# One transformer layer on one core: another scratch place for a norm's squares, late modulation sums made and read in the middle of a product, and block 0's output sums on VectorE

## The chip, the cores and the metric

The kernel runs on one core of a Trainium2 chip. A core has five engines that run side by side, each through its own list of instructions in order: TensorE (PE in the profile, with PEld for the loading of its weights), VectorE (DVE), ScalarE (ACT), GpSimd (POOL) and SyncE (SP), which here only issues transfers (DMA). An instruction waits until the semaphores that it names have been reached, and everything behind it on its engine waits too. Matmuls write their results into PSUM, a small memory of banks; a bank holds 128 x 512 numbers of 32 bits. All else lies in SBUF, in 128 partitions.

The metric is the time of one execution on the device in microseconds (us).

## The reference

The reference is an encoder trunk with one layer: 2048 tokens of 1024 numbers, a mixer and a feed-forward network (FFN), each between two RMS norms, with shift, scale and gate computed from a vector c. With one layer the mixer is stick-breaking attention with 16 heads of 64.

```python
def stick_breaking_mixer(h, w_qkv, w_o):
    qkv = (h @ w_qkv).reshape(b, s, 3, N_HEADS, HEAD_DIM)
    q, k, v = qkv[:, :, 0], qkv[:, :, 1], qkv[:, :, 2]
    for q0 in range(0, s, SB_BLOCK):
        ...
        z = jnp.einsum('bthd,bshd->bhts', q[:, q0:end], k[:, :end]).astype(jnp.float32) * scale
        ...
        sp = jnp.where(mask, jax.nn.softplus(z), 0.0)
        rest = lax.cumsum(sp, axis=3, reverse=True)
        log_a = jnp.where(mask, z - rest, -jnp.inf)
        a = jnp.exp(log_a).astype(v.dtype)
        outs.append(jnp.einsum('bhts,bshd->bthd', a, v[:, :end]))
    o = jnp.concatenate(outs, axis=1).reshape(b, s, D_MODEL)
    return o @ w_o
...
    mod_all = jnp.einsum('bd,lde->lbe', jax.nn.silu(c), ada_w) + ada_b[:, None]
        sh_m, sc_m, gt_m, sh_f, sc_f, gt_f = jnp.split(mod_all[i][:, None, :], 6, axis=-1)
        h = modulate(rms_norm(x, norm_g[i, 0]), sh_m, sc_m)
        y = stick_breaking_mixer(h, sb_w_qkv[r], sb_w_o[r])
        x = x + gt_m * rms_norm(y, norm_g[i, 1])
        h = modulate(rms_norm(x, norm_g[i, 2]), sh_f, sc_f)
        y = swiglu_ffn(h, ffn_w_in[i], ffn_w_out[i])
        x = x + gt_f * rms_norm(y, norm_g[i, 3])
```

The modulation vector has six segments of 1024, numbered 0 to 5: shift, scale and gate of the mixer, then of the FFN. Segments 0 and 1 are needed at the very start, 2 (the mixer's gate) only after the attention, 3 and 4 before the FFN, and 5 at the end.

## The kernel before

Every product of float32 numbers is made of three matmuls: each operand is split into a high and a low part, and high·high, high·low and low·high are summed in one bank (`mm3`, L192 to L194). The tokens are taken in 4 blocks of 512, the heads in 8 pairs p. Names carry these numbers: `pj5_3_0` is the product of pair 5, block 3, kind 0 (0 queries, 1 keys, 2 values), `xT2_0` belongs to block 2.

The order of the work on PE, ACT, DVE and POOL is the order in which the program is written, with generators that are stepped in turn. SP's order of transfers is chosen by a scheduler. The stages by time are: loads, the modulation's first segments and the first products (to about 60 us); projections and attention, interleaved (to about 1390); the output projection (to about 1530); the FFN (to the end).

*The first norm.* The tokens of a block are loaded in four tiles x (`x_load`, L319). ACT squares each tile (`x_square`, L183) and sums the squares along the way; only the sums are used, the squares themselves go to a scratch place (`junk`). DVE then scales the tiles (L340), PE transposes them (xT, L366) and ACT writes the modulated result (hf, L387) from the bank that the transposes filled. Blocks 1 and 3 square in place. Block 2 writes its squares to four tiles xj of the tag "wraw", of which there are two places; the keys and queries of an early pair (kn, qn) have stood in the same places, from which they are stored to memory (k_park L502, q_park L516).

*The attention.* A slot of the loop makes one row of scores: z (L588), its exponentials on ACT (L605, L607), a cumulative sum along the row on DVE (the scans w, L617 and L622), a difference on POOL (a, L629) with carries c (L628), a transpose on PE (t, L639), the split into high and low parts aT (L649 on ACT, L655 on DVE), and the product with the values (o, L667). Between these, PE makes the projections pj of a later block: a product has 8 slices k, three matmuls each, and its result is split by ACT and DVE (kn and qn, L490 and L491) or transposed (vT L530, vt L536, v L540 and L541). One pool of three banks, tag "acc", holds the products pj, the sums o, the transposes vt and the sums ap of the next paragraph; t has two banks, z three.

*Late modulation.* `late_modulation` is a generator that loads the weights of a segment in chunks (aw, L225, into "wraw" places), multiplies and adds them on DVE into aacc, waits `settle` steps, and sums aacc over the partitions by matmuls with a tile of ones into a bank ap. For a gate (segments 2 and 5) it loads rows of constants (gr), adds ap and multiplies on DVE (L296, L297), and stores the row; else it adds to columns (shift L249 or scale). In the attention it runs from slot 120 on, every second slot, for segments 2, 3 and 4; for segment 5 it runs in the FFN, with its tiles in "aT" places.

*Output sums.* The result of the attention is written to memory in two parts (high and low sums). `lead_in` does block 0's share of the output projection's preparation while the attention still runs: each of 8 tiles is loaded (`o_load`, op), its parts are added (`o_add`, of, L1082), and the sum is split (`o_prep`, ohl, L1089 on ACT and L1090 on DVE). It takes tiles 0 to 5 at about 1262 to 1302 us, and tiles 6 and 7 at about 1331 to 1338.

Of the kernel before, what the change touches and what calls it, by code (L numbers as in the profile page):

```python
# [9 lines left out]
F32 = mybir.dt.float32  # L10
F32R = mybir.dt.float32r
AF = mybir.ActivationFunctionType
ALU = mybir.AluOpType
# [107 lines left out]
def hybrid_trunk_kernel(  # L121
# [136 lines left out]

    def late_modulation(segs, tag, n, ahead, waits, pool, ptag, acc_tag="tmp", rows_tag="wraw", settle=3, pace=1):

# [9 lines left out]
        for at, (seg, half, k0) in enumerate(chunks):  # L270
# [13 lines left out]
            if k0 + n < KC:  # L284
                continue
            for _ in range(settle):
                yield
            ps = pool.tile([P, BT], F32, name=f"ap{seg}_{half}", tag=ptag)
            if seg in (2, 5):
                g = seg // 3  # L290
                rows = att.tile([P, 2, BT], F32, name=f"gr{g}_{half}", tag=rows_tag, bufs=BUFS[rows_tag])
                nc.sync.dma_start(rows, gate_consts[g : g + 1, half].to_broadcast((P, 2, BT)))
                nc.tensor.matmul(ps, ones, acc, start=True, stop=True)
                for _ in range(3):
                    yield
                nc.vector.tensor_tensor(rows[:, 0], ps, rows[:, 0], op=ALU.add)  # L296
                nc.vector.tensor_tensor(rows[:, 0], rows[:, 0], rows[:, 1], op=ALU.mult)  # L297
                nc.sync.dma_start(gate_rows[g, :, half * BT : (half + 1) * BT], rows[:, 0])
            else:
                ada_cols([acc], ps, half)  # L300
                yield
                sl = slice(4 * half, 4 * half + 4)
# [25 lines left out]
    def x_square(b, i):  # L328
        junk = x_tiles[b, i]
        if b == 0:  # L330
            junk = x_norm[b, i] = att.tile([P, D], F32, name=f"xn{b}_{i}", tag="kt", bufs=BUFS["kt"])
        elif b == 2:
            junk = att.tile([P, D], F32, name=f"xj{b}_{i}", tag="wraw", bufs=BUFS["wraw"])
        x_rstd[b, i] = rms_scale(att, x_tiles[b, i], f"n0_{b}_{i}", junk=junk)
# [115 lines left out]
    def project(at):  # L450
# [10 lines left out]
        def product(t):  # L461
# [7 lines left out]
            for k in range(KC):  # L469
# [11 lines left out]
                if ahead and k == 6:  # L481
                    split_weights(p + 1, t)
                mm3(acc, (w[0][:, k], w[1][:, k]), (h[k][:, 0], h[k][:, 1]), k == 0, k == KC - 1)
                yield
            return acc
# [465 lines left out]
    products(1, 7)  # L951
    late = late_modulation((2, 3, 4), "wraw", 2, 0, 3, accps, "acc")

# [124 lines left out]
    def o_add(b, k):  # L1078
        parts = o_parts.pop((b, k))
        o = att.tile([P, BT], F32, name=f"of{b}_{k}", tag="tmp", bufs=BUFS["tmp"])  # L1080
        eng = nc.vector if b else nc.gpsimd
        eng.tensor_tensor(o, parts[:, 0], parts[:, 1], op=ALU.add)  # L1082
        o_sum[b, k] = o
# [697 lines left out]
```

## Time and profile before

| | |
|---|---|
| median of 3 runs | 2841.5 us (2839.93, 2841.5, 2845.77) |
| the profiled execution | 2840.45 us |
| its span, first to last instruction | 2838.2 us |
| PE busy | 2798.2 us (99%) |
| DVE busy | 2022.4 us (71%) |
| ACT busy | 1630.7 us (57%) |
| POOL busy | 1282.5 us (45%) |
| mean granted clock of PE | 0.998 |

A row of the timeline gives start, length, engine, line, operation, output and inputs (buffer numbers left out), and the number of instructions that were put together. A bracket at its end gives how long the engine stood idle before it, and what ended the wait. A row of the windows gives a stretch of time, its length, the busy time (and instructions) of PE, PEld, DVE, ACT and POOL, then PE's granted clock, the share of DMA engines at work, and GB/s. A row of grouped instructions gives the shortest, median and longest duration in ns. Busy times count overlapping instructions once.

### The profile page before, as it was taken

What the parts mean: (1) busy time and instruction counts of PE and PEld (TensorE: products, weight loads), DVE (VectorE), ACT (ScalarE), POOL (GpSimd) and SP (SyncE); (2) the same over time, 40 slices, a digit from 0 to 9 for tenths busy, and PEclk for the clock granted to TensorE, in tenths of its full rate; (3) what the DMA queues carried; (4) which work ended last, traced back from release to release, by engine and by line L of the source; (5) the groups of instructions that cost most, each with busy time, mean ns of one, the idle gap of its engine ahead of it and who ended that gap; (6) DMA issues with size and microseconds to landing.
All of it is one profiled execution on the core that took longest, in us unless ns stands there. A gap on an engine that the chain in (4) does not pass through costs nothing.

```text
span 2838.2 us, 41766 instructions
## 1 busy us (share of the span) xinstructions
PE 2798.2 (99%) x13821; PEld 2331.5 (82%) x13821; DVE 2022.4 (71%) x2833; ACT 1630.7 (57%) x3271; POOL 1282.5 (45%) x2032
## 2 busy tenths in 40 slices
PE   9899999999999999999999999999999999999998
PEld 7688888888888888887888888888888888888887
DVE  7788888888888888888866766655775665123376
ACT  5787777787787877877645533333433333322243
POOL 1575666676576655657411222221222222544454
PEclk9999999999999999999999999999999999999999
DMA  9774556656665635546288644334453334545575
GB/s 378 275 226 164 186 163 220 212 179 226 193 210 187 214 115 178 196 134 231 85 304 308 207 138 152 123 94 160 137 178 108 112 108 164 192 140 155 180 226 187
DMA packets 239785, 521.03 MB, mean 184 GB/s; under 512 B 22481, under 2 KB 108497, under 8 KB 222674
## 3 DMA queue, kind: packets, MB, share of 16 engines
q1 hardware_dynamic: 239570, 518.38, 56.2%
q8 instruction: 109, 1.79, 0.3%
q14 instruction: 106, 0.87, 0.1%
HBM read 351.04 MB, written 118.49 MB: 165 GB/s over the span
## 4 chain that ended last, share of the span: by engine, by line
PE 88%; DVE 4%; issue 2%; DMA 2%; ACT 2%; POOL 1%; SPq 0%; DVEq 0%; POOLq 0%; ACTq 0%
PE s L192 9%; PE s L193 9%; PE s L194 9%; PE z L588 8%; PE o L667 8%; PE t L639 8%; PE pj L192 5%; PE pj L194 5%; PE pj L193 5%; PE o L194 5%; PE o L193 5%; PE o L192 5%; PE y L194 2%; PE y L192 2%; PE y L193 2%
## 5 line engine op out<-in xcount | busy, mean ns | idle before, releaser
L629 POOL TENSOR_TENSOR a<-a,w 128x512 f32<-128x512 f32 (+3 forms) x640 | 622.1, 972 | 218.9 <-DVE w L622 128.6
L622 DVE TENSOR_TENSOR_SCAN w<-z,c,begin 128x512 f32<-128x512 f32 x384 | 489.2, 1278 | 83.7 <-ACT z L607 62.0
L192 PE MATMUL s<-r,l 128*128 128x512 f32 x1232 | 481.4, 391 | 1.5 <-ACT p L1456 0.9
L194 PE MATMUL s<-r,l 128*128 128x512 f32 x1232 | 479.6, 389 | 0.0
L193 PE MATMUL s<-r,l 128*128 128x512 f32 x1232 | 479.4, 389 | 0.0
L605 ACT ACTIVATE a<-z 128x512 f32<-128x512 f32 (+3 forms) x640 | 347.1, 542 | 170.0 <-PE z L588 137.3
L667 PE MATMUL o<-aT,v 128*128 128x512 f32 (+3 forms) x1280 | 385.3, 382 | 0.1
L655 DVE TENSOR_TENSOR aT<-t,aT 128x512 fp32r<-128x512 f32 (+3 forms) x640 | 358.4, 593 | 24.3 <-ACT aT L649 23.7
L588 PE MATMUL z<-kt,qt 128*128 128x512 f32 (+3 forms) x1280 | 363.6, 365 | 0.0
L649 ACT CAST aT<-t 128x512 fp32r<-128x512 f32 (+3 forms) x640 | 313.9, 533 | 73.6 <-PE t L639 63.5
L607 ACT ACTIVATE z<-z 128x512 f32<-128x512 f32 (+3 forms) x640 | 344.8, 539 | 0.0
L1520 POOL TENSOR_TENSOR one<-p,p 128x512 f32<-128x512 f32 x44 | 70.6, 1606 | 574.5 <-issue 321.8
L192 PE MATMUL pj<-ht,w 128*128 128x512 f32 x768 | 309.3, 403 | 5.4 <-issue 1.4
L639 PE MATMUL t<-begin,a 128*128 128x128 f32 x2176 | 295.1, 273 | 13.3 <-DVE aT L655 12.0
L639 PEld LDWEIGHTS t<-begin,a 128*128 128x128 f32 x2176 | 255.2, 140 | 63.4 <-DVE aT L655 14.2
L193 PE MATMUL pj<-ht,w 128*128 128x512 f32 x768 | 301.7, 393 | 0.9 <-DVE ht L767 0.2
L194 PE MATMUL pj<-ht,w 128*128 128x512 f32 x768 | 301.9, 393 | 0.0
L192 PEld LDWEIGHTS s<-r,l 128*128 128x128 f32 x1232 | 231.2, 188 | 51.2 <-ACT p L1456 1.7
L194 PEld LDWEIGHTS s<-r,l 128*128 128x128 f32 x1232 | 231.2, 188 | 48.8 <-DVE l L1374 0.4
L193 PEld LDWEIGHTS s<-r,l 128*128 128x128 f32 x1232 | 231.3, 188 | 48.0 <-issue 0.5
L617 DVE TENSOR_TENSOR_SCAN w<-z,begin 128x128 f32<-128x128 f32 (+3 forms) x256 | 208.6, 817 | 76.9 <-ACT z L607 65.5
L588 PEld LDWEIGHTS z<-kt,qt 128*128 128x128 f32 x1280 | 230.9, 189 | 37.5 <-DVE w L617 0.2
(181 smaller groups left out, 4871.5 us busy)
## 6 DMA issues: line engine op xcount, KB each, us to landing
ht<-h_s SPq DMA_DIRECT2D x108, 1024.0 KB, 8.3
wi<-in_win SPq DMA_DIRECT2D x86, 512.0 KB, 3.9
qt<-qn SPq DMA_DIRECT2D x124, 256.0 KB, 4.8
ol_qt<-act_s SPq DMA_DIRECT2D x56, 512.0 KB, 3.7
act_s<-S SPq DMA_DIRECT2D x66, 256.0 KB, 4.0
br<-in_wout SPq DMA_DIRECT2D x66, 256.0 KB, 3.3
h_s<-ht SPq DMA_DIRECT2D x16, 1024.0 KB, 9.0
o_s<-os SPq DMA_DIRECT2D x128, 128.0 KB, 2.6
```

What stands on the lines that cost most here:

```text
L192: nc.tensor.matmul(acc, lhs[0], rhs[0], start=first, stop=False, **kw)
L193: nc.tensor.matmul(acc, lhs[0], rhs[1], start=False, stop=False, **kw)
L194: nc.tensor.matmul(acc, lhs[1], rhs[0], start=False, stop=last, **kw)
L588: nc.tensor.matmul(z[:, :n], q[:, e, part, r * P : (r + 1) * P], k[:, e, :n], start=part == 0, stop=part == 1,)
L605: nc.scalar.activation(a[:, :n], z[:, :n], AF.Sigmoid, scale=QK_SCALE)
L607: nc.scalar.activation(z[:, :n], z[:, :n], AF.Sigmoid, scale=-QK_SCALE)
L622: nc.vector.tensor_tensor_scan(rest[:, rev], left[:, rev], begin[:, :BT][:, rev], initial=carries[r], op0=ALU.mult, op1=ALU.bypass,)
L629: nc.gpsimd.tensor_tensor(a[:, :n], a[:, :n], rest[:, 1 : n + 1], op=ALU.mult)
L639: nc.tensor.transpose(pt[:, rb * P : (rb + 1) * P], weighed[i, rb][:, j * P : (j + 1) * P], ident)
L649: nc.scalar.copy(hl[:, 0, t0:], pt[:, t0:])
L655: nc.vector.tensor_tensor(hl[:, 1, t0:], pt[:, t0:], f32(hl[:, 0, t0:]), op=ALU.subtract)
L667: nc.tensor.matmul(acc[:, t0:], lhs, hl[:, part, t0:], start=sc == qb and j == 0 and part == 0, stop=sc == 0 and j == 3 and part == 1,)
```

## The change

Three edits, and what each does:

1. The squares of block 2 all write to one tile xj2, of tag "v" (seven places) instead of four tiles of tag "wraw".
2. In late modulation the rows of constants for a gate are asked for before the settling steps, not after. With `inside` given (segments 2 to 4, in the attention), the generator then waits until the product that is being made stands in slice 2, 3 or 4 (`slice_at` holds the last slice made). The matmuls into ap and the reading of ap follow each other without a step between. In the FFN (segment 5) there is no `inside`, but the steps between matmul and reading are gone too.
3. The output sums of block 0 run on DVE, as those of the other blocks did already.

```diff
-    def late_modulation(segs, tag, n, ahead, waits, pool, ptag, acc_tag="tmp", rows_tag="wraw", settle=3, pace=1):
+    slice_at = [0]
+
+    def late_modulation(segs, tag, n, ahead, waits, pool, ptag, acc_tag="tmp", rows_tag="wraw", settle=3, pace=1, inside=None):
...
             if k0 + n < KC:
                 continue
+            g = seg // 3
+            if seg in (2, 5):
+                rows = att.tile([P, 2, BT], F32, name=f"gr{g}_{half}", tag=rows_tag, bufs=BUFS[rows_tag])
+                nc.sync.dma_start(rows, gate_consts[g : g + 1, half].to_broadcast((P, 2, BT)))
             for _ in range(settle):
+                yield
+            while inside and slice_at[0] not in inside:
                 yield
             ps = pool.tile([P, BT], F32, name=f"ap{seg}_{half}", tag=ptag)
             if seg in (2, 5):
-                g = seg // 3
-                rows = att.tile([P, 2, BT], F32, name=f"gr{g}_{half}", tag=rows_tag, bufs=BUFS[rows_tag])
-                nc.sync.dma_start(rows, gate_consts[g : g + 1, half].to_broadcast((P, 2, BT)))
                 nc.tensor.matmul(ps, ones, acc, start=True, stop=True)
-                for _ in range(3):
-                    yield
                 nc.vector.tensor_tensor(rows[:, 0], ps, rows[:, 0], op=ALU.add)
...
                 ada_cols([acc], ps, half)
-                yield
                 sl = slice(4 * half, 4 * half + 4)
...
         elif b == 2:
-            junk = att.tile([P, D], F32, name=f"xj{b}_{i}", tag="wraw", bufs=BUFS["wraw"])
+            if i == 0:
+                x_places["junk"] = att.tile([P, D], F32, name=f"xj{b}", tag="v", bufs=BUFS["v"])
+            junk = x_places["junk"]
...
                 mm3(acc, (w[0][:, k], w[1][:, k]), (h[k][:, 0], h[k][:, 1]), k == 0, k == KC - 1)
+                slice_at[0] = k
                 yield
...
-    late = late_modulation((2, 3, 4), "wraw", 2, 0, 3, accps, "acc")
+    late = late_modulation((2, 3, 4), "wraw", 2, 0, 3, accps, "acc", inside=range(2, 5))
...
     def o_add(b, k):
...
-        eng = nc.vector if b else nc.gpsimd
-        eng.tensor_tensor(o, parts[:, 0], parts[:, 1], op=ALU.add)
+        nc.vector.tensor_tensor(o, parts[:, 0], parts[:, 1], op=ALU.add)
```

The first edit moves no instruction. What the other two move is seen in the order of instructions; the lines of the changed kernel are 4 or 5 higher than those of before (L667 is L672, L1082 is L1086).

PE at the first of the late sums, ap2_0 (pair 2's keys of block 3 are the product beside it, w the split weights, h the normed tokens), before:

```order
L192 MATMUL pj2_3_1_5353<-ht2_3_0_5345,w2_1_3231 128x512
L193 MATMUL pj2_3_1_5353<-ht2_3_0_5345,w2_1_3231 128x512
L194 MATMUL pj2_3_1_5353<-ht2_3_0_5345,w2_1_3231 128x512
L293 MATMUL ap2_0_5369<-aacc2_0_4292,ones_68 128x512
L667 MATMUL o1_1_3_5031<-aT39_1_5297,v1_0_2009 128x512 x2
L588 MATMUL z41_2_5375<-kt2_0_3866,qt2_0_4022 128x384 x2
L192 MATMUL pj2_3_1_5353<-ht2_3_0_5345,w2_1_3231 128x512
L193 MATMUL pj2_3_1_5353<-ht2_3_0_5345,w2_1_3231 128x512
L194 MATMUL pj2_3_1_5353<-ht2_3_0_5345,w2_1_3231 128x512
L639 MATMUL t40_0_5381<-begin_62,a40_0_5232 128x128
```

and with the change:

```order
L298 MATMUL ap2_0_5413<-aacc2_0_4289,ones_68 128x512
L672 MATMUL o1_1_3_5028<-aT39_3_5358,v1_0_2006 128x512 x2
L593 MATMUL z42_0_5427<-kt2_1_4401,qt2_1_4593 128x128 x2
L192 MATMUL pj2_3_1_5352<-ht2_3_1_5346,w2_1_3228 128x512
L193 MATMUL pj2_3_1_5352<-ht2_3_1_5346,w2_1_3228 128x512
L194 MATMUL pj2_3_1_5352<-ht2_3_1_5346,w2_1_3228 128x512
L644 MATMUL t40_2_5433<-begin_62,a40_2_5277 128x128
L644 MATMUL t40_2_5433<-begin_62,a40_3_5300 128x128
L644 MATMUL t40_3_5436<-begin_62,a40_3_5300 128x128
L672 MATMUL o2_0_0_5450<-aT40_0_5392,v2_0_4237 128x512 x2
```

A tile of ht holds two slices, so the sum stood between slices 0 and 1 of pj2_3_1, and now stands between slices 2 and 3. Behind it, within ten rows, another row of o (o2_0_0) begins, which takes a bank of the same pool. On DVE the reading of ap2_0, which came three steps later, is now written directly behind the sum.

PE at the second, ap2_1, before (pj3_1_2 is the product that follows pj3_1_0):

```order
L192 MATMUL pj3_1_0_6690<-ht3_1_3_6521,w3_0_5674 128x512
L193 MATMUL pj3_1_0_6690<-ht3_1_3_6521,w3_0_5674 128x512
L194 MATMUL pj3_1_0_6690<-ht3_1_3_6521,w3_0_5674 128x512
L293 MATMUL ap2_1_6841<-aacc2_1_5753,ones_68 128x512
L667 MATMUL o2_0_3_6767<-aT52_3_6779,v2_3_5965 128x128 x2
L588 MATMUL z55_0_6848<-kt2_0_3866,qt2_3_5730 128x512 x2
L192 MATMUL pj3_1_0_6690<-ht3_1_3_6521,w3_0_5674 128x512
L193 MATMUL pj3_1_0_6690<-ht3_1_3_6521,w3_0_5674 128x512
L194 MATMUL pj3_1_0_6690<-ht3_1_3_6521,w3_0_5674 128x512
L192 MATMUL pj3_1_2_6862<-ht3_1_0_6515,w3_2_5864 128x512
```

and with the change:

```order
L192 MATMUL pj3_1_0_6689<-ht3_1_2_6518,w3_0_5673 128x512
L193 MATMUL pj3_1_0_6689<-ht3_1_2_6518,w3_0_5673 128x512
L194 MATMUL pj3_1_0_6689<-ht3_1_2_6518,w3_0_5673 128x512
L298 MATMUL ap2_1_6790<-aacc2_1_5631,ones_68 128x512
L672 MATMUL o2_0_3_6766<-aT52_1_6722,v2_3_5964 128x384 x2
L593 MATMUL z54_2_6797<-kt2_1_4401,qt2_3_5730 128x512 x2
L192 MATMUL pj3_1_0_6689<-ht3_1_2_6518,w3_0_5673 128x512
L193 MATMUL pj3_1_0_6689<-ht3_1_2_6518,w3_0_5673 128x512
L194 MATMUL pj3_1_0_6689<-ht3_1_2_6518,w3_0_5673 128x512
L644 MATMUL t53_0_6803<-begin_62,a53_0_6642 128x128
```

The sum stood between slices 6 and 7, with the next product directly behind; it now stands between slices 4 and 5.

DVE where block 0's sums are prepared (w are scans, aT the low parts of the transposed rows, qn a split product), before:

```order
L655 TENSOR_TENSOR aT143_0_16509<-t143_0_16490,aT143_0_16509 128x512
L1090 TENSOR_TENSOR ohl0_0_16516<-of0_0_16430,ohl0_0_16516 128x512
L491 TENSOR_TENSOR qn7_2_16524<-pj7_2_0_16340,qn7_2_16524 128x512
L655 TENSOR_TENSOR aT143_1_16536<-t143_1_16495,aT143_1_16536 128x512
L617 SCALAR_TENSOR_TENSOR w144_3_16539<-z144_3_16521,begin_62 128x512
L622 SCALAR_TENSOR_TENSOR w145_0_16566<-z145_0_16550,c144_0_16455,begin_62 128x512
L655 TENSOR_TENSOR aT143_2_16573<-t143_2_16556,aT143_2_16573 128x512
L655 TENSOR_TENSOR aT143_3_16587<-t143_3_16561,aT143_3_16587 128x512
L622 SCALAR_TENSOR_TENSOR w145_1_16590<-z145_1_16578,c144_1_16479,begin_62 128x512
L1090 TENSOR_TENSOR ohl0_1_16601<-of0_1_16514,ohl0_1_16601 128x512
L622 SCALAR_TENSOR_TENSOR w145_2_16621<-z145_2_16606,c144_2_16506,begin_62 128x512
```

and with the change:

```order
L660 TENSOR_TENSOR aT143_0_16506<-t143_0_16487,aT143_0_16506 128x512
L1086 TENSOR_TENSOR of0_1_16511<-op0_1_16356 128x512
L1094 TENSOR_TENSOR ohl0_0_16513<-of0_0_16427,ohl0_0_16513 128x512
L496 TENSOR_TENSOR qn7_2_16521<-pj7_2_0_16337,qn7_2_16521 128x512
L660 TENSOR_TENSOR aT143_1_16533<-t143_1_16492,aT143_1_16533 128x512
L622 SCALAR_TENSOR_TENSOR w144_3_16536<-z144_3_16518,begin_62 128x512
L627 SCALAR_TENSOR_TENSOR w145_0_16563<-z145_0_16547,c144_0_16452,begin_62 128x512
L660 TENSOR_TENSOR aT143_2_16570<-t143_2_16553,aT143_2_16570 128x512
L660 TENSOR_TENSOR aT143_3_16584<-t143_3_16558,aT143_3_16584 128x512
L627 SCALAR_TENSOR_TENSOR w145_1_16587<-z145_1_16575,c144_1_16476,begin_62 128x512
L1086 TENSOR_TENSOR of0_2_16596<-op0_2_16425 128x512
L1094 TENSOR_TENSOR ohl0_1_16598<-of0_1_16511,ohl0_1_16598 128x512
```

Two sums, of0_1 and of0_2, now stand among DVE's rows, each one row ahead of the split ohl of the sum before it; the others of the first six stand likewise. POOL held them before, between the carries c and the differences a:

```order
L629 TENSOR_TENSOR a143_3_16422<-a143_3_16422,w143_3_16421 128x512
L1082 TENSOR_TENSOR of0_0_16430<-op0_0_16269 128x512
L602 MEMSET w144_0_16449 128x1
L628 COPY c144_0_16455<-w144_0_16449 128x1
L629 TENSOR_TENSOR a144_0_16450<-a144_0_16450,w144_0_16449 128x128
L602 MEMSET w144_1_16473 128x1
L628 COPY c144_1_16479<-w144_1_16473 128x1
L629 TENSOR_TENSOR a144_1_16474<-a144_1_16474,w144_1_16473 128x256
L602 MEMSET w144_2_16500 128x1
L628 COPY c144_2_16506<-w144_2_16500 128x1
L629 TENSOR_TENSOR a144_2_16501<-a144_2_16501,w144_2_16500 128x384
L1082 TENSOR_TENSOR of0_1_16514<-op0_1_16359 128x512
```

There of0_0 and of0_1 are gone, and nothing takes their place.

## The prediction

> **What bounds the kernel now.** I read the head of the page first, then the waits of TensorE (PE), then the timeline and the windows around the three places that the edits touch.
>
> ```profile
> span 2838.2 us, 41766 instructions
> PE 2798.2 (99%) x13821; PEld 2331.5 (82%) x13821; DVE 2022.4 (71%) x2833; ACT 1630.7 (57%) x3271; POOL 1282.5 (45%) x2032
> PE 88%; DVE 4%; issue 2%; DMA 2%; ACT 2%; POOL 1%; SPq 0%; DVEq 0%; POOLq 0%; ACTq 0%
> ```
>
> The reader is to see that PE is busy for all but 40.0 us of the span (2838.2 less 2798.2). No edit takes a matmul away, so all that can be won is a piece of these 40 us, and time in which PE is busy at a lower clock. Where the 40 us lie stands in the waits of PE:
>
> ```profile
> PE t L639 <- DVE aT L655: 12.0, 15, 2.3
> PE xT L366 <- DVE x L340: 5.2, 4, 4.6
> ```
>
> The columns are the total, the number of waits and the longest. The first row belongs to the attention's pipeline, which nothing here touches on purpose. The second is one wait of 4.6 us, at the first edit.
>
> **The change, part 1: block 2's squares.**
>
> ```profile
> 64.03 0.56 ACT L540 CAST v<-vt 128x512 fp32r<-128x512 f32 x1
> 71.66 1.06 ACT L183 ACTIVATE xj<-x 128x1024 f32<-128x1024 f32 x1 [7.06 <-issue]
> 66.02 0.53 SPq L502 DMA_DIRECT2D k_park<-kn  x1
> k_park<-kn SPq DMA_DIRECT2D x1, 512.0 KB, 5.6
> 77.52 2.73 DVE L340 TENSOR_SCALAR x<-x,n_rstd 128x1024 f32<-128x1024 f32 x4
> 78.31 0.48 PE L366 MATMUL xT<-begin,x 128*128 128x128 f32 x1 [4.60 <-DVE x L340]
> 73.60:78.30 4.70, 0.11 (x2) 0.00 (x0) 2.26 (x7) 3.76 (x8) 1.78 (x5) 0.89 1.01 420
> 78.30:84.00 5.70, 5.12 (x15) 3.57 (x16) 3.67 (x6) 0.78 (x1) 0.00 (x0) 0.50 0.99 370
> ```
>
> ACT stands idle for 7.06 us ahead of the first square. The scratch tile xj lies in a "wraw" place that holds kn until its store k_park has landed: 66.02 + 5.6 = 71.6, and the square starts at 71.66. Four squares, four scales on VectorE (DVE) and then the transposes xT follow; PE stands from 73.7 to 78.31. In the window after that (its last three columns are PE's granted clock, the DMA share and GB/s) PE runs at 0.50, so its 5.12 us of work there would be about 2.6 at full clock. By the Trainium skill ("TensorE: Matmul & The Clock Gate", the table of the two states), an idle window of some 3.4 us sets the clock to half; the trace agrees, 4.60 us of idling and then 0.50.
>
> Now one tile of tag "v" takes all four squares; nothing is stored from it. What it still needs is x2 itself:
>
> ```profile
> 48.21 0.33 SPq L319 DMA_DIRECT2D x<-in_x  x1
> x<-in_x SPq DMA_DIRECT2D x1, 512.0 KB, 12.3
> x<-in_x SPq DMA_DIRECT2D x1, 512.0 KB, 13.1
> ```
>
> The last of block 2's loads is issued at 48.21 and lands 13.1 us later, at 61.3. ACT is free at 64.6; four squares of 1.06 with a cast of 0.56 among them end around 69.4, and the scales (2.73) around 72 to 73, before PE comes to xT at 73.7. The stall can go whole: 4.6 us, and with it the halved clock, 2.6 to 3.3 us (to the end of the slow stretch a little past 84). That is the upper end, −7.9.
>
> What is late next is block 3's x, which ACT squares in order ahead of block 2's later work:
>
> ```profile
> 82.11 2.59 SPq L319 DMA_DIRECT2D x<-in_x  x4
> x<-in_x SPq DMA_DIRECT2D x4, 512.0 KB, 7.5
> x<-in_x SPq DMA_DIRECT2D x1, 512.0 KB, 6.3
> 90.56 1.05 ACT L183 ACTIVATE x<-x 128x1024 f32<-128x1024 f32 x1
> 92.59 0.77 ACT L387 ACTIVATE hf<-xT,mod,g_eff 128x512 f32<-128x512 f32 x1
> ```
>
> The four loads are issued from 82.11 to 84.7 and land 7.5 us on in the median; the first, at 6.3 us, is there at 88.4. ACT squares it at 90.56, so it can move ahead by 2.2 us only, if the load does not move. I take it that it doesn't: the two windows above show a DMA share of 1.01 and 0.99, so the queue is full of bytes that nobody removes. Behind that square, on ACT, stands hf at 92.59, which frees the bank of the next xT: PE, having come 7.9 us early, waits there instead, and may lose its clock a second time. So the gain at ACT is 90.56 − 88.4 = 2.2. The lower end is 0 (the wait moves whole). I take **−2.2**, because the order on ACT is fixed and its row is the nearest.
>
> **Part 2: the late modulation's sums.** These waits of PE stand at the places where an "ap" bank is made, or is held while a product wants the bank (bracket: idle before, and what ended it):
>
> ```profile
> 431.88 0.70 PE L293 MATMUL ap<-aacc,ones 128*128 128x512 f32 x1 [0.71 <-DVE v L541]
> 446.87 0.50 PE L192 MATMUL pj<-ht,w 128*128 128x512 f32 x1 [0.20 <-DVE gr L296]
> 544.08 0.50 PE L192 MATMUL pj<-ht,w 128*128 128x512 f32 x1 [1.40 <-DVE qn L491]
> 758.59 0.47 PE L192 MATMUL pj<-ht,w 128*128 128x512 f32 x1 [0.24 <-DVE shift L249]
> 860.93 0.47 PE L192 MATMUL pj<-ht,w 128*128 128x512 f32 x1 [1.42 <-issue]
> 960.51 0.50 PE L192 MATMUL pj<-ht,w 128*128 128x512 f32 x1 [0.87 <-DVE kn L491]
> 437.50 1.79 DVE L617 TENSOR_TENSOR_SCAN w<-z,begin 128x512 f32<-128x512 f32 x2 [0.60 <-ACT z L607]
> 438.46 0.73 PE L667 MATMUL o<-aT,v 128*128 128x512 f32 x2
> 446.15 0.67 DVE L296 TENSOR_TENSOR gr<-ap,gr 128x512 f32<-128x512 f32 x1
> ```
>
> "acc" has three banks, for products, o, vt and ap. An ap that is made as a product ends leaves the next product without a bank until the finished one has been read; an ap that waits three yields for its add holds its bank for as long. The changed order makes ap in slices 2 to 4 (the quoted orders of PE) and reads it at once, so these six waits lose their cause: 0.71 + 0.20 + 1.40 + 0.24 + 1.42 + 0.87 = 4.84. Against that stands one wait that I find in the new order: the first ap comes ahead of the o of 438.46, which takes its bank only after the add on DVE, and DVE is in a pair of scans until about 438.6 (437.50, x2). The add takes 0.67 (row 446.15), so it ends about 439.3, and the o, due at 438.9 behind the new matmul, is some 0.4 late. −4.84 + 0.4 = **−4.4**. Ends: −4.8 if DVE's order gives the add room, and −1 if most of the new reads queue behind a scan as this one does (six reads, some 0.6 each). SP issues the loads of gates and of modulation weights earlier, past loads of the products' weights; I cost that at nothing, since DMA ends 2% of the chain in all and the wait rows of PE name no weight load. Should one weight load come late, PE would stand for a piece of its landing, 5 to 13 us by the rows above. The same edit in the FFN (segment 5) has next to nothing to win:
>
> ```profile
> 2121.56 0.50 PE L192 MATMUL s<-r,l 128*128 128x512 f32 x1 [0.50 <-DVE p L1512]
> ```
>
> This is the only wait of PE near its sums, and the sums move by a few slices to one side of it: 0, give or take 0.5.
>
> **Part 3: block 0's output sums.**
>
> ```profile
> L1082 DVE TENSOR_TENSOR of<-op x24: 679/682/693, 1398.9 to 1499.1; 128x512 f32<-128x512 f32 x24
> L1082 POOL TENSOR_TENSOR of<-op x8: 1291/1506/1747, 1264.3 to 1334.6; 128x512 f32<-128x512 f32 x8
> L1090 DVE TENSOR_TENSOR ohl<-of,ohl x32: 661/684/1561, 1267.9 to 1503.0; 128x512 fp32r<-128x512 f32 x32
> 1262.00:1300.00 38.00, 36.83 (x200) 30.41 (x200) 33.56 (x45) 30.59 (x68) 29.51 (x56) 1.00 0.71 244
> 1283.95 0.66 PE L639 MATMUL t<-begin,a 128*128 128x128 f32 x4 [0.33 <-DVE aT L655]
> 1334.35 0.85 DVE L1090 TENSOR_TENSOR ohl<-of,ohl 128x512 fp32r<-128x512 f32 x1 [1.15 <-ACT ohl L1089]
> 1335.85 0.55 PE L639 MATMUL t<-begin,a 128*128 128x128 f32 x3 [1.20 <-DVE aT L655]
> ```
>
> Eight adds of 1.51 us leave GpSimd (POOL), which bounds nothing there, and eight of 0.68 come onto DVE: 5.5 us. Six of them, 4.1 us, fall into 1262 to 1300, where DVE is busy 33.56 of 38 us, which leaves 4.4; two fall at 1331 to 1336, into the 1.15 us in which DVE waits for ACT's ohl, itself waiting for POOL's slow sum, so there I cost nothing. In the first stretch the idle time of DVE would be all but used up. PE's slack behind DVE is small there (0.33 of stall at 1283.95). One thing speaks in favour: an ohl that runs beside a POOL sum takes up to 1.56 instead of 0.68, and that goes. I take **+0.7** of 4.1, with ends −0.7 (only the slow ohl goes) and +3 (most of the 4.1 reaches PE).
>
> A rule against this stands in the Trainium skill, "GPSIMD Engine Reference", section "Specifications": POOL shares its ports to SBUF with DVE, and contends with DVE instructions that have two SBUF inputs. The sums are such instructions, and POOL is busy 29.51 of 38 us there; the 0.68 is measured where POOL does little. The 1.56 of the slowest ohl agrees with the rule, and by it the eight sums would cost 8 × 1.56 = 12.5 us: rival C.
>
> **Sum.** −2.2 − 4.4 + 0 + 0.7 = −5.9. The profiled execution took 2840.45 us (span 2838.2), 1.05 below the median of 2841.5 of the runs shown; against the median the forecast is **2835.6**, 0.21% faster. About 0.2%, 5.7 us, is what can be told from no change, so the bound lies at 2835.8, all but on my forecast.
>
> **The rivals.**
> A. *The first stall goes whole.* If block 3's loads land earlier, or ACT's wait for them does not reach PE, part 1 is −7.9: 2841.5 − 7.9 − 4.4 + 0.7 = 2829.9. For it: ACT's order leaves PE other work (products of pair 0 and 1). Against it: a DMA share of 1.
> B. *The first stall only moves.* PE reaches block 3's xT 5 us early, waits for the load for more than the 4.6 us of before, and gets half its clock again: part 1 is 0, and the time 2837.8. For it: the idle time stays in one piece. Against it: the 2.2 us at ACT.
> C. *Slower: the output sums hold up DVE.* Each sum takes 1.56 beside POOL's work, and DVE has 4.4 us free for six of them. If all 12.5 us reach PE: −2.2 − 4.4 + 12.5 = +5.9, 2847.4. It decides from 6.6 us on (slower than before), and from 12.3 on by over 0.2%. For it: DVE would be over-full, 33.56 + 9.4 > 38. Against it: two sums fill an idle stretch, and ohl gets shorter by as much as it is freed.
> D. *The late sums don't do what they say.* The wait for a bank is paid by the next o or product behind a scan on DVE, six times 0.7: part 2 is −0.2, and the time 2839.8. For it: the wait that I found at 438.9. Against it: the other five places show none in the order.
>
> **How the numbers follow.** Chances: forecast 0.48 (own range 2832 to 2838: part 2 between its ends, part 3 between −0.7 and +3), A 0.16, B 0.11, D 0.10, C 0.15. The predicted time is that of the forecast, 2835.6. The range takes in A with a margin of the run's spread, B and D with part 3's upper end: 2828.5 to 2843, and leaves out C. The bound of 0.2% cuts the forecast's own range nearly in half, 0.27 to 0.21. Faster: 0.27 + 0.16 = 0.43; same: 0.21 + 0.11 + 0.10 = 0.42; slower: 0.15.
>
> **What would show it.** Part 1: the first square near 64.6, no wait of 4.6 us before xT, clock 1.00 in 74 to 84, and a new wait of PE or a longer one around 86 to 92, ended by ACT's hf. If that wait is missing, A; if the clock falls to 0.5 there, B. Part 2: the six waits gone, at most one of about 0.4 at 439 (less what the start wins). Part 3: PE's stalls in 1262 to 1300 longer by under 1 us in all, of on DVE at 0.7 to 1.1; with of near 1.56 and DVE without a gap, C. I am wrong if stalls appear where DVE had none, above all t waiting for aT in 1285 to 1300.

## The result, and the profile after

The changed kernel takes 2835.72 us (median of 9 runs, 2834.4 to 2842.68) against 2841.5 us before: a ratio of 0.9979, 95% interval 0.9971 to 0.9988. The forecast was 2835.6, and the moved time lies about on the bound of 0.2%, as forecast.

The head of the page of the profiled execution after the change:

```profile
span 2832.7 us, 41794 instructions
PE 2795.5 (99%) x13821; PEld 2333.0 (82%) x13821; DVE 2029.6 (72%) x2841; ACT 1634.6 (58%) x3271; POOL 1273.0 (45%) x2024
PE 90%; DVE 3%; ACT 2%; DMA 2%; issue 2%; POOL 1%; SPq 0%; DVEq 0%; POOLq 0%; ACTq 0%
```

Eight instructions have moved from POOL (2032 to 2024) to DVE (2833 to 2841). PE stands still for 37.2 us instead of 40.0 and is busy 2.7 us less with the same 13821 matmuls.

The waits of PE after the change (total, number, longest):

```profile
PE t L644 <- DVE aT L660: 15.7, 18, 2.3
PE xT L370 <- ACT hf L391: 4.8, 1, 4.8
```

The wait of 4.6 us for DVE's scaled x is gone, and one of 4.8 us for ACT's hf has come. The attention's own wait, t for aT, has grown from 12.0 to 15.7 us. So each gain has a loss beside it, and the waits alone don't tell the balance. To get it, the same instruction of PE is looked up in two timelines, and the starts are subtracted; what changes from one place to the next is what the stretch between cost or saved. Against the profiled execution of before (minus is ahead):

| stretch of PE's work (us of before) | changed kernel |
|---|---|
| start to 45 | +1.5 |
| 45 to 140 (squares) | −2.9 |
| 140 to 1250 (late sums, segments 2 to 4) | −4.4 |
| 1260 to 1345 (output sums) | +1.9 |
| 1420 to 1600 | −1.2 |
| 2000 to 2200 (late sums, segment 5) | −0.3 |

The first row has no change in it: the instructions up to 45 us are the same ones. Nor has the row from 1420 to 1600: every other kernel below gains 0.2 to 1.6 us there too, so most of it belongs to the execution of before.

**The start.** The timelines of ACT, SP and PE around the squares, after:

```profile
65.98 1.06 ACT L183 ACTIVATE xj<-x 128x1024 f32<-128x1024 f32 x1
79.44 6.20 SPq L321 DMA_DIRECT2D x<-in_x  x4
88.67 1.06 ACT L183 ACTIVATE x<-x 128x1024 f32<-128x1024 f32 x1 [4.69 <-DMA x<-in_x]
91.54 1.11 PE L370 MATMUL xT<-begin,x 128*128 128x128 f32 x4 [4.78 <-ACT hf L391]
```

and the windows there:

```profile
73.60:78.30 4.70, 4.70 (x29) 4.03 (x28) 2.99 (x5) 2.16 (x4) 0.00 (x0) 1.00 1.02 424
78.30:84.00 5.70, 5.41 (x31) 4.25 (x30) 4.45 (x8) 4.29 (x10) 1.31 (x5) 1.00 0.98 328
84.00:88.00 4.00, 2.73 (x16) 2.21 (x16) 1.67 (x3) 0.00 (x0) 0.69 (x1) 1.00 1.01 307
88.00:96.00 8.00, 4.46 (x15) 3.78 (x16) 5.16 (x12) 7.33 (x14) 3.18 (x6) 0.60 0.99 402
```

The squares begin without a wait, at 65.98 instead of 71.66, and PE works at full clock through 73.6 to 84, where it stood or ran at half clock before. Then ACT waits 4.69 us for block 3's first tile, its square starts at 88.67 (90.56 before), PE waits 4.78 us behind it, and the granted clock falls to 0.60 in 88 to 96. The old wait has come back 13 us later and nearly as long (4.78 for 4.60). What is gained is what the load leaves: 1.9 us at ACT's square, and by 140 us 2.9 in PE's drift.

**The late sums.** The grouped additions into aacc (shortest, median and longest in ns), before:

```profile
L235 DVE SCALAR_TENSOR_TENSOR aacc<-aw,c_act,aacc x56: 721/727/1786, 354.4 to 2116.5; 128x512 f32<-128x512 f32 x56
```

and after:

```profile
L235 DVE SCALAR_TENSOR_TENSOR aacc<-aw,c_act,aacc x56: 721/730/2731, 353.0 to 2110.2; 128x512 f32<-128x512 f32 x56
```

All waits of PE between 425 and 1250 us after the change, where the six waits for banks stood before:

```profile
PE t L644 <- DVE aT L660: 3.4, 6, 0.8
PE t L644 <- POOL w L220: 0.6, 1, 0.6
```

None of the six is left. Two of the additions in the timelines of DVE and POOL after the change, and the new waits of PE:

```profile
453.11 2.38 POOL L220 TENSOR_TENSOR w<-wr,w 128x1024 fp32r<-128x1024 f32 x1
453.98 2.06 DVE L235 SCALAR_TENSOR_TENSOR aacc<-aw,c_act,aacc 128x512 f32<-128x512 f32 x1
469.99 2.39 POOL L220 TENSOR_TENSOR w<-wr,w 128x1024 fp32r<-128x1024 f32 x1
470.20 2.73 DVE L235 SCALAR_TENSOR_TENSOR aacc<-aw,c_act,aacc 128x512 f32<-128x512 f32 x1
458.74 0.66 PE L644 MATMUL t<-begin,a 128*128 128x128 f32 x4 [0.54 <-DVE aT L660]
474.43 1.25 PE L644 MATMUL t<-begin,a 128*128 128x128 f32 x8 [0.69 <-DVE aT L660]
479.27 0.94 PE L644 MATMUL t<-begin,a 128*128 128x128 f32 x6 [0.37 <-DVE aT L660]
```

An addition that takes 0.73 us by itself took 2.06 and 2.73 us where it met POOL's split of weights (2.38 and 2.39 us): both ended 0.55 us behind the split, about as if they had begun when it was over. The late sums' other steps had moved, and with them these two. PE lost 2.3 us between 450 and 500, and still gained 4.4 from 140 to 1250.

**The output sums.** Grouped, after the change:

```profile
L1086 DVE TENSOR_TENSOR of<-op x32: 666/684/1468, 1257.2 to 1494.2; 128x512 f32<-128x512 f32 x32
```

in the timelines of DVE, POOL and PE:

```profile
1269.87 1.39 POOL L634 TENSOR_TENSOR a<-a,w 128x512 f32<-128x512 f32 x1 [0.97 <-DVE w L627]
1270.23 1.58 DVE L1094 TENSOR_TENSOR ohl<-of,ohl 128x512 fp32r<-128x512 f32 x1
1289.52 1.10 POOL L634 TENSOR_TENSOR a<-a,w 128x512 f32<-128x512 f32 x1
1289.70 1.47 DVE L1086 TENSOR_TENSOR of<-op 128x512 f32<-128x512 f32 x1
1265.11 0.65 PE L644 MATMUL t<-begin,a 128*128 128x128 f32 x4 [0.72 <-DVE aT L660]
1279.41 0.66 PE L644 MATMUL t<-begin,a 128*128 128x128 f32 x4 [0.93 <-DVE aT L660]
1292.29 0.33 PE L644 MATMUL t<-begin,a 128*128 128x128 f32 x1 [1.19 <-DVE aT L660]
```

and the window that answers to 1262 to 1300 of before:

```profile
1257.00:1295.00 38.00, 34.45 (x187) 28.46 (x186) 35.65 (x49) 28.44 (x64) 21.30 (x47) 1.00 0.71 243
```

PE waits 2.84 us for aT in three places, where it waited 0.33 before; DVE is busy 35.65 us of 38 instead of 33.56. The slow split ohl of before (1.56) is gone, and another (1.58) has come. PE's drift grows by 2.4 us up to 1330, over tiles 0 to 5, and falls by 0.5 behind it, at tiles 6 and 7.

### The profile page after: what moved, and what is told of

The parts are those of the page before. It is cut to its first block, busy times and chain, and to the rows that moved or that the text cites. A ratio compares the mean times of both kernels' runs of the same rounds, so it can differ in the third digit from the quotient of the medians.

```text
span 2832.7 us, 41794 instructions
## 1 busy us (share of the span) xinstructions
PE 2795.5 (99%) x13821; PEld 2333.0 (82%) x13821; DVE 2029.6 (72%) x2841; ACT 1634.6 (58%) x3271; POOL 1273.0 (45%) x2024
## 3 DMA queue, kind: packets, MB, share of 16 engines
q8 instruction: 109, 1.79, 0.3%
## 4 chain that ended last, share of the span: by engine, by line
PE 90%; DVE 3%; ACT 2%; DMA 2%; issue 2%; POOL 1%; SPq 0%; DVEq 0%; POOLq 0%; ACTq 0%
PE s L192 9%; PE s L194 9%; PE s L193 9%; PE o L672 8%; PE z L593 8%; PE t L644 8%; PE pj L192 6%; PE pj L194 6%; PE pj L193 6%; PE o L194 4%; PE o L192 4%; PE o L193 4%; PE y L194 2%; PE y L192 2%; PE y L193 2%
## 5 line engine op out<-in xcount | busy, mean ns | idle before, releaser
L672 PE MATMUL o<-aT,v 128*128 128x512 f32 (+3 forms) x1280 | 385.2, 382 | 0.0
L644 PE MATMUL t<-begin,a 128*128 128x128 f32 x2176 | 295.6, 273 | 16.8 <-DVE aT L660 15.7
```

The source lines that it names most:

```text
L644: nc.tensor.transpose(pt[:, rb * P : (rb + 1) * P], weighed[i, rb][:, j * P : (j + 1) * P], ident)
L672: nc.tensor.matmul(acc[:, t0:], lhs, hl[:, part, t0:], start=sc == qb and j == 0 and part == 0, stop=sc == 0 and j == 3 and part == 1,)
```

## The experiments

All ratios are against the kernel before, on the same chip, with their 95% intervals. Since a part is worth about a thousandth, the drift of PE by stretches, as in the table above, says more than a ratio. It comes from one profiled execution of each kernel, and for the same edit it mostly repeats from kernel to kernel:

| kernel | ratio | 45–140 | 140–1250 | 1260–1345 |
|---|---|---|---|---|
| squares alone | 0.9998 (0.9989–1.0006) | −5.3 | +0.1 | 0.0 |
| squares alone, again | 0.9996 (0.9987–1.0005) | −3.0 | 0.0 | 0.0 |
| late sums alone | 0.9987 (0.9979–0.9996) | −0.5 | −4.4 | 0.0 |
| output sums alone | 1.0009 (1.0000–1.0017) | −0.8 | +0.1 | +1.9 |
| squares and late sums | 0.9972 (0.9961–0.9983) | −3.6 | −4.3 | 0.0 |
| … and block 3's squares later | 0.9986 (0.9977–0.9994) | −2.0 | −4.4 | 0.0 |
| … and additions apart | 0.9958 (0.9946–0.9971) | −3.2 | −8.7 | 0.0 |
| … and both | 0.9967 (0.9958–0.9976) | −2.0 | −8.8 | 0.0 |
| squares, late sums, output sums 0, 6, 7 | 0.9979 (0.9968–0.9989) | −3.8 | −4.4 | −0.5 |
| squares, late sums, no accumulation | one run | −3.1 | −6.1 | 0.0 |
| squares, additions apart, output sums 0, 6, 7 | 0.9965 (0.9953–0.9978) | −4.0 | −8.7 | −0.5 |
| additions apart, without squares | 0.9977 (0.9967–0.9987) | +0.1 | −8.7 | 0.0 |

### Squares alone

```diff
-            junk = att.tile([P, D], F32, name=f"xj{b}_{i}", tag="wraw", bufs=BUFS["wraw"])
+            if i == 0:
+                x_places["junk"] = att.tile([P, D], F32, name=f"xj{b}", tag="v", bufs=BUFS["v"])
+            junk = x_places["junk"]
```

> Only the squares' scratch place is changed. Theory (the gain is limited by block 3's loads): PE's wait of 4.6 us before block 2's transposes goes, a new one of 4 to 5 us before a later xT comes with a stretch at half clock, and 2.2 to 3.3 us remain: ratio 0.9988 to 0.9992, about 2838.5 against 2841.5. Rival A (the stall goes whole): -7.9 us, ratio 0.9972. Rival B (it only moves): ratio 1.000.

Measured: 2840.18 against 2839.99 us, 0.9998 (0.9989 to 1.0006): no gain that can be told. Its profiled execution was already 6.0 us late at 45 us, before the edit has begun. Windows of this execution at its start:

```profile
20.00:24.00 4.00, 4.00 (x16) 3.39 (x16) 2.79 (x4) 1.72 (x2) 0.00 (x0) 0.50 1.03 410
24.00:32.00 8.00, 8.00 (x30) 6.71 (x28) 2.92 (x5) 2.88 (x4) 0.00 (x0) 0.50 1.03 409
```

the second of them with squares and late sums together:

```profile
24.00:32.00 8.00, 8.00 (x42) 6.40 (x42) 6.75 (x12) 4.71 (x6) 0.00 (x0) 1.00 1.03 410
```

and PE's wait for block 3 in the execution of squares alone:

```profile
94.91 1.12 PE L368 MATMUL xT<-begin,x 128*128 128x128 f32 x4 [3.62 <-ACT hf L389]
```

The same instructions, behind the same two waits of PE (1.08 and 0.23 us), ran at half clock in one execution and at full clock in the other. From 45 to 140 us PE then gains 5.3 us, more than any kernel that started within 2 us of before. Of this, 0.9 us come between 118 and 140, where the clock stayed full behind a wait that halved it in the kernel before (last section). Some 1.4 us of the delay were taken back, since PE waits less for block 3's load with a late start (3.62 us here, 4.78 in the changed kernel). That isn't so in every late start: with three of the output sums on VectorE, below, PE was 7.5 us late at 45 and gained 3.7.

> The squares' scratch place alone, once more. By the traces (PE 2.4 to 3.3 us ahead at 140 us where the start is alike): ratio 0.9988 to 0.9992. Rival B (the stall only moves): 1.000.

Again: 2838.17 against 2840.17, 0.9996 (0.9987 to 1.0005). The start is alike here (+1.2 at 45 us), and PE is 3.0 us nearer at 140. Neither ratio excludes my theory's 0.9988 to 0.9992 or rival B's 1.000. By traces the four kernels with the old place drift by 0, −0.5, −0.8 and +0.1 from 45 to 140 (mean −0.3); of those with the new place and block 3's squares where they were, the ones that started within 2 us of before drift by −2.9, −3.0, −3.1, −3.2, −3.6 and −4.0 (mean −3.3). The last two owe 0.9 us each to the full clock behind that same wait, as above; without it the mean is −3.0. The squares are worth about 3 us by the traces; the ratios can't tell it.

### Late sums alone

All of the late modulation's edits, the squares and the sums as before; at the heart of it:

```diff
             for _ in range(settle):
+                yield
+            while inside and slice_at[0] not in inside:
                 yield
             ps = pool.tile([P, BT], F32, name=f"ap{seg}_{half}", tag=ptag)
...
                 nc.tensor.matmul(ps, ones, acc, start=True, stop=True)
-                for _ in range(3):
-                    yield
                 nc.vector.tensor_tensor(rows[:, 0], ps, rows[:, 0], op=ALU.add)
```

> Only the late modulation is changed. Theory: the six waits of 4.84 us go, and what the trace of the changed kernel shows as new (two slow adds into aacc beside GpSimd's weight splits, about 2.5 us lost between 453 and 481 us) is paid here too: net -4 to -4.8 us, ratio 0.9983 to 0.9986. Rival D (the late sums only move the waits): ratio 0.9999.

Measured: 2836.59 against 2839.99, 0.9987 (0.9979 to 0.9996), −3.4; in the trace −4.4 from 140 to 1250 and −0.3 at segment 5, with the additions at 2.06 and 2.72 us and the same three new waits. Rival D (0.9999) is outside the interval. The six waits of the forecast are gone, and the loss beside the weight splits is paid here too.

### Output sums alone

```diff
-        eng = nc.vector if b else nc.gpsimd
-        eng.tensor_tensor(o, parts[:, 0], parts[:, 1], op=ALU.add)
+        nc.vector.tensor_tensor(o, parts[:, 0], parts[:, 1], op=ALU.add)
```

> Only the output sums of block 0 go from GpSimd to VectorE. By the drift between the two traces it costs: +1.5 to +2 us, ratio 1.0005 to 1.0007. By the prediction's term +0.7: ratio 1.0002. Rival C (VectorE over-full): +12.5 us, ratio 1.0044.

Measured: 2842.52 against 2839.99, 1.0009 (1.0000 to 1.0017), +2.5; in the trace +1.9, just as in the changed kernel. Rival C's 1.0044 is out; so is my own +0.7, by the trace.

### Without the output sums

The changed kernel with `o_add` as before:

```diff
-        nc.vector.tensor_tensor(o, parts[:, 0], parts[:, 1], op=ALU.add)
+        eng = nc.vector if b else nc.gpsimd
+        eng.tensor_tensor(o, parts[:, 0], parts[:, 1], op=ALU.add)
```

> The changed kernel without its third edit (output sums of block 0 back on GpSimd). If the third edit costs 1.5 to 2 us, this is 2833.8 to 2834.3, ratio 0.9973 to 0.9975, and it beats both kernels; if the sums cost nothing, it is 2835.7 as the changed kernel, ratio 0.998.

Measured: 2831.84 against 2839.99, 0.9972 (0.9961 to 0.9983). The ratio is 0.0007, 2 us, below the changed kernel's 0.9979; the two intervals overlap, but by the drift (0.0 against +1.9) it is the third edit that costs the 2 us. This kernel beats the one before by its ratio, and the changed one by the drift.

### Block 3's squares later

```diff
-    (3, 1, 0): [("cols", 3), ("square", 3, 0)],
-    (3, 1, 1): [("square", 3, 1)],
-    (3, 1, 2): [("square", 3, 2), ("spread", 3, 0)],
...
+    (3, 1, 0): [("cols", 3)],
+    (3, 1, 2): [("square", 3, 0)],
+    (3, 1, 3): [("square", 3, 1)],
+    (3, 1, 4): [("square", 3, 2), ("spread", 3, 0)],
...
```

> Squares and late modulation changed, sums left on GpSimd, and besides the squares of block 3 stand two slices later on ScalarE, behind two more hf. Theory (in the changed kernel PE waits some 4.8 us because ScalarE stands in order behind a square whose tile has not landed): that wait goes, and with it part of the stretch at half clock, 3 to 5 us below squares and late modulation alone, ratio 0.995 to 0.996. Rival (the transfers themselves are the bound up to 100 us): another wait for a transfer or for block 3's norm takes its place, ratio 0.997 as without it.

Measured: 0.9986 (0.9977 to 0.9994), no better than without it (0.9972, with an interval that overlaps), and 1.7 us worse in the drift from 45 to 140, of which 0.9 is the clock behind the wait near 125 us, full there and halved here. The 0.995 to 0.996 of my theory are outside the interval. This profiled execution started 4.2 us late, at half clock. The run with both edits, below, started 7.7 us late and gained 2.0 us as well, where three of the output sums on VectorE, 7.5 us late with the squares in their old order, gained 3.7. So the later squares are worse by 0.7 to 1.7 us, and nowhere better. The new wait of PE in this kernel's timeline, and the window behind it:

```profile
101.04 0.66 PE L594 MATMUL z<-kt,qt 128*128 128x128 f32 x2 [3.75 <-DMA qt<-qn]
```

```profile
101.00:104.00 3.00, 2.96 (x10) 2.68 (x11) 0.90 (x2) 0.94 (x3) 1.13 (x2) 0.50 0.98 300
```

The wait for ACT is gone, and PE stands 3.75 us for the queries of the next block instead, with its clock at 0.50 behind. With both edits the same wait for qt is 3.95 us. The rival stated for this run holds: up to 100 us the transfers set the pace, whichever of them PE meets first. My theory, that ScalarE's order costs the time, falls.

### Additions apart from the weight splits

```diff
             for i in range(n):
+                while inside and slice_at[0] in (6, 7):
+                    yield
                 ada_add(acc, loaded[at], k0, i, k0 + i == 0)
```

> Squares and late modulation changed, sums left on GpSimd, and the additions into aacc are not written while the product stands in its last two slices, where GpSimd splits weights. Theory (two additions of 2.06 and 2.73 us beside a weight split cost PE about 2.5 us near 453 to 481 us): no addition above 1.7 us there, and 1.5 to 2.5 us less, ratio about 0.9965. Rival (the loss there has another cause, such as the earlier reads of the gate): the three new waits of PE stay, ratio 0.9972.

Measured: 2828.14 against 2840.73, 0.9958 (0.9946 to 0.9971). The grouped additions in this kernel, and the first row of PE's waits:

```profile
L235 DVE SCALAR_TENSOR_TENSOR aacc<-aw,c_act,aacc x56: 724/727/1787, 353.0 to 2103.7; 128x512 f32<-128x512 f32 x56
```

```profile
PE t L646 <- DVE aT L662: 10.8, 12, 2.3
```

No addition of the attention takes more than 1.4 us (the 1787 ns is one of segment 5, which the edit doesn't touch), the three waits between 453 and 481 are gone, and the late sums are worth 8.7 us instead of 4.4. I had expected 1.5 to 2.5 us more; of the 4.4 that came, 2.8 are there by 500 us, where the two additions and the three waits stood. The rest comes by 930, past additions of 1.2 to 1.4 us beside POOL, of which the changed kernel has three and this one has one; that these make up the rest isn't shown, since the rule moves the other steps of the generator too.

> Both of the foregoing together. If both causes hold and are apart in time, their gains add: 4.5 to 7.5 us below squares and late modulation alone, ratio 0.994 to 0.9955.

Both together: 0.9967 (0.9958 to 0.9976). The gains don't add as expected, since the later squares give none; the late sums' part repeats, 8.8 us by the drift.

### Three of the output sums on VectorE

```diff
+        eng = nc.vector if b or k in (0, 6, 7) else nc.gpsimd
```

> Squares and late modulation changed, and of block 0's output sums only tiles 0, 6 and 7 go to VectorE, where it has idle time; tiles 1 to 5 stay on GpSimd. Theory (the cost of the third edit arises where VectorE is full, with tiles 1 to 5): no cost, as with all sums on GpSimd, between 1260 and 1345 us PE stays within 0.3 us. Rival (each sum costs alike, 1.9 us for eight): 0.7 us more than with all on GpSimd.

Measured: 0.9979 (0.9968 to 0.9989); this profiled execution had a start at half clock (+7.5 us at 45 us), and from 1260 to 1345 PE gains 0.5 us, a little outside the 0.3 that I had allowed, all of it at tiles 6 and 7. PE's wait for aT between 1262 and 1300 us, with three sums on DVE and, in the second row, with none:

```profile
1283.31 0.66 PE L644 MATMUL t<-begin,a 128*128 128x128 f32 x4 [0.33 <-DVE aT L660]
```

```profile
1275.89 0.66 PE L644 MATMUL t<-begin,a 128*128 128x128 f32 x4 [0.33 <-DVE aT L660]
```

Tile 0 costs nothing and tiles 6 and 7 gain 0.5 us, so the cost of the third edit, 2.4 us up to 1330, comes from tiles 1 to 5, which stand where DVE is busy 35.65 of 38 us. That is a difference between kernels; no run moved these five alone.

### One SBUF input instead of two

```diff
-        if first:
-            nc.vector.tensor_scalar(acc, w[:, i], scale, None, op0=ALU.mult)
-        else:
-            nc.vector.scalar_tensor_tensor(acc, w[:, i], scale, acc, op0=ALU.mult, op1=ALU.add)
+        nc.vector.tensor_scalar(acc, w[:, i], scale, None, op0=ALU.mult)
```

> Squares and late modulation changed, sums on GpSimd; the additions into aacc are left out: each step of the late modulation only multiplies its weights (one SBUF input instead of two), in the same place of VectorE's order, so the modulation comes out as its last chunk alone. Theory (two SBUF inputs on VectorE wait for GpSimd's whole weight split): no step over 0.6 us even beside a weight split, and the 2.4 us that PE loses between 453 and 481 are gone. Rival (any VectorE instruction waits there, or the loss has another cause): two steps of 1.8 to 2.5 us near 452 and 468, and the loss stays.

The steps without accumulation, grouped, and the timeline of the two beside POOL's weight splits:

```profile
L232 DVE TENSOR_SCALAR aacc<-aw,c_act x64: 455/462/2486, 347.3 to 2103.9; 128x512 f32<-128x512 f32 x64
```

```profile
451.22 2.39 POOL L220 TENSOR_TENSOR w<-wr,w 128x1024 fp32r<-128x1024 f32 x1
452.09 1.83 DVE L232 TENSOR_SCALAR aacc<-aw,c_act 128x512 f32<-128x512 f32 x1
467.85 2.38 POOL L220 TENSOR_TENSOR w<-wr,w 128x1024 fp32r<-128x1024 f32 x1
468.06 2.49 DVE L232 TENSOR_SCALAR aacc<-aw,c_act 128x512 f32<-128x512 f32 x1
```

The theory as I put it falls: an instruction with one SBUF input tile, 0.46 us by itself, takes 1.83 and 2.49 us, ending 0.3 us behind the split. What waits is not only the kind with two inputs. That the waiting costs PE is seen in the drift: the loss between 450 and 500 is 1.6 us here and 2.4 with the additions, with the same places and 0.27 us less of work each.

### The parts put together

> Squares and late modulation changed, additions into aacc kept out of a product's last two slices, and output sums 0, 6 and 7 of block 0 on VectorE. The drifts of the parts add: start -3, late modulation -8.7, sums -0.5: 12 us below the kernel before, ratio 0.9957.

Squares, additions apart and output sums 0, 6 and 7 on DVE: 2829.43 against 2840.17, 0.9965 (0.9953 to 0.9978), five runs. The profiled execution is the shortest of all (span 2824.1), and the drifts add as expected, but the interval doesn't part it from 0.9958 without the three sums. Either beats the kernel before by its ratio, and the changed one by the drift.

> Late modulation changed, with its additions kept out of the last two slices; squares of block 2 in the old place, sums on GpSimd. If the late modulation is worth 8.7 us by itself: ratio 0.9969; the difference to the same kernel with the squares changed (0.9958) is the squares' part, 2 to 4 us by the traces.

Additions apart without the squares: 0.9977 (0.9967 to 0.9987). The late sums are again worth 8.7 us in the drift, 6.5 by the ratio. Against 0.9958 with the squares that leaves 0.0019, 5 us, for the squares, with an uncertainty of some 4.5 us; the drifts say 3.

## Why the prediction was right

**The sum.** −5.9 was forecast, −5.8 measured between the medians. Of the terms, by drift: squares −2.2 forecast, about −3 shown (−2.9 in the changed kernel); late sums −4.4 forecast, −4.4 shown and −0.3 at segment 5 (0 ± 0.5); output sums +0.7 forecast, +1.9 shown. The last term was too small by 1.2, within its end of +3, and the first too small by 0.7 to 1.1 the other way: the total was luckier than its parts. And the interval of the ratio, some −8.2 to −3.4 us, is wider than these errors, so that the two totals agree to a tenth is luck as well.

**Part 1, as forecast.** The wait goes, PE meets block 3's load, and the gain is what that load leaves: ACT's square was forecast for 88.4 and started at 88.67. The step "if the load does not move" held in these two executions: the first of block 3's loads was issued 2.7 us earlier (79.44 against 82.11) and took 9.2 us instead of 6.3, so it landed at 88.65 against 88.43, with a DMA share of 0.98 to 1.02 all the way. The size of the term, 2.2, is the time for which the landed tile lay unread before, and it was read from one execution. In the four executions with the old place it is 2.1 to 2.9 us (with additions apart, without the squares, the load landed at 87.84 and the square began at 90.71), and in the three kernels with the new place that started within 0.2 us of before the square begins at 87.4 to 87.7, some 3 us earlier.

The sign that I gave for rival B (a clock at 0.5 in that place) was seen, 0.60 in 88 to 96, with the wait of 4.78 us, and yet B's price was wrong: PE has done the work that stood behind the old wait before it meets the new one, and by its drift 2.9 us are gained when both are over. Rival A is out. A slip without consequence: the last of block 2's loads was not the one of 48.21; another was issued at 49.41 and landed at 62.52, still before ACT came free at 64.6. That the queue of transfers bounds this stretch, not ACT's order, was argued in the forecast from the DMA share; the two runs with block 3's squares later, in which PE waits 3.75 and 3.95 us for another transfer instead, bear it out.

**Part 2, right in its sum, not in its terms.** The six waits are gone. The wait of 0.4 us at 439, the one loss that I named, did not come:

```profile
435.46 0.67 DVE L299 TENSOR_TENSOR gr<-ap,gr 128x512 f32<-128x512 f32 x1
436.27 0.71 PE L672 MATMUL o<-aT,v 128*128 128x512 f32 x2
```

The addition ended at 436.13, behind one scan and not two, and the row of o began at 436.27 without a wait. (The pair of scans that I quoted ends at 439.29, 437.50 and 1.79, and not at 438.6; read rightly, it would have made the loss about 1 us.) In its place stood a loss that I had not looked for, 2.3 us between 450 and 500, from two additions beside weight splits. I had costed what the moved sums do to the banks and to the loads; the additions into aacc, which shift by a few steps with the generator, I left out. The gain in the six places, in turn, is larger than the 4.84 us that their brackets list; with the collisions avoided the late sums are worth 8.7. Three additions of before that took 1.28 to 1.64 us belong to that difference; how the rest of it is made up the runs don't settle.

**Part 3, mechanism right, size off.** The term was 0.7 of 4.1 us, on the ground that most of it falls into DVE's idle time and that a slow ohl goes. That was too favourable by 1.7 us in the first stretch: the six sums there cost PE 2.4 us, tile 0 none of it, and the two at 1331 to 1336, which I had put at nothing, gave 0.5 back. And the slow ohl did not go, it moved: an instruction of DVE still meets POOL's difference a (ohl 1.58 beside one of 1.39, of 1.47 beside one of 1.10). By rival C's price of 1.56 each the eight sums would take 12.5 us; six took 0.67, 1.12, 0.67, 0.93, 0.67 and 1.47, and the 1.9 us that they cost PE in all stay far below the 6.6 from which C decides. The Trainium skill's "GPSIMD Engine Reference", section "Specifications", names contention between GpSimd and VectorE; these rows agree that it is there, and show that it depends on what POOL is doing at that moment.

## What to carry to other kernels

When a change shifts a generator or a planner's steps, list every instruction that shifts with it, not only the ones it is about, and look what stands beside them on GpSimd and VectorE: here a rule that kept 0.7 us additions away from 2.4 us weight splits was worth another 4.3 us by the drift, as much as the whole late-sum edit had given. Where transfers never pause, look at the next one before a wait is called won: here the wait came back at the next load, and the gain was about the time for which that load's tile had lain unread, which could be read from the old timeline to within a microsecond. And a part that is worth a thousandth is better measured by the drift of one instruction between two timelines than by the time of the whole.

## What the runs showed of the hardware

An instruction of DVE that reads SBUF beside a long instruction of POOL can wait until that one has ended: 0.73 us became 2.06 and 2.73, and with one input 0.46 became 1.83 and 2.49, beside weight splits of 2.4 us. In the changed kernel all ten additions into aacc of over 1 us ended 0.55 us behind the POOL instruction that had begun before them, whether that one took 1.09 or 2.40 us. Where the addition began first, it was POOL that was held up:

```profile
492.97 0.73 DVE L235 SCALAR_TENSOR_TENSOR aacc<-aw,c_act,aacc 128x512 f32<-128x512 f32 x1
493.20 1.46 POOL L634 TENSOR_TENSOR a<-a,w 128x512 f32<-128x512 f32 x1 [1.15 <-DVE w L627]
```

Eighteen differences a of 128x512 that began 0.23 to 0.27 us behind an addition took 1.42 to 1.46 us, where 1.09 is usual, and these eighteen additions took 0.72 to 0.74. So the one to be late is the one that begins second, and an addition's delay can be read from what is left of the POOL instruction. The section of the Trainium skill named above gives the two kinds that contend, a 2-port mode or two SBUF inputs; that the one-input multiplication is in such a mode no run here shows directly.

PE's clock in the first 40 us differs between executions with the same instructions: 0.50 in 20 to 32 us with squares alone, 1.00 in the changed kernel. The four executions with the lower clock there were 4.2 to 7.7 us late at 45 us, the others at most 1.7. The Trainium skill, "TensorE: Matmul & The Clock Gate", in Part 1, "What's actually happening", says that the window of the clock gate runs freely and that the same kernel differs from run to run; the rows here agree that it differs, and don't show the window. Nor is an idle time of some 3.4 us needed, as the forecast had it from the Trainium skill. Behind the same wait of PE, 2.28 us in the kernel before and 2.27 with squares alone, the clock was halved in the one and stayed full in the other:

```profile
126.00:128.00 2.00, 2.00 (x9) 1.81 (x8) 1.41 (x5) 0.66 (x2) 1.61 (x5) 0.50 0.83 262
128.00:130.00 2.00, 1.89 (x13) 1.37 (x13) 1.75 (x5) 1.80 (x5) 1.95 (x7) 1.00 0.67 197
```

The clock goes with the scatter of the times: squares alone, again, took 2835.89 us in the run with the highest mean clock (0.999) and 2842.33 in the one with the lowest (0.995). A scatter of 6 us is twice what the squares are worth, so their gain can't be read from the ratios.
